# One layer of a hybrid encoder on one core: PSUM tiles cut to single banks, first head loads, combination steps and fillers re-timed

## The chip, the core and the metric

The kernel runs on one core of one Trainium2 chip. The metric is device time in microseconds of one launch; the kernel before has a median of 1358.91 us over three runs (1358.9 to 1362.09). The engines are called by the names of the profile: PE (matmuls; PEld is its weight load), DVE, ACT, POOL, and SP, whose queue SPq issues every DMA of this kernel (all go through one helper, line 119, in the order in which the program names them).

## The reference

For 1024 tokens and a model width of 1024 (fp32):

```python
h = rmsnorm(x)
proj = h @ w_in                       # split into mla | dilated q, k, v, z | gates
a_out = mla_attention(...)            # 8 heads, full softmax over 1024 keys
y_mla = (a_out * silu(z_mla)) @ w_o_mla
d_out = dilated_mixture(...)          # 3 groups x 8 heads, windows (128,1), (512,4), (2048,16)
y_dil = (d_out * silu(z_dil)) @ w_o_dil
merged = sigmoid(g_mla + b) * y_mla + sigmoid(g_dil + b) * y_dil
out = rmsnorm(x + merged @ w_out)
```

In the dilated mixture the three groups' outputs of one head are added with weights that come from a softmax over their log-denominators. That weighting is called the combination below.

## The kernel before, in words

Every fp32 product is made of three fp32r products of a high and a low part: `mm3` (lines 122 to 125) issues them, and `split` (lines 127 to 130) makes the parts, high on ACT, low on POOL or DVE.

**Stages.** Up to 528 us of the profiled execution the kernel computes the normed input, the latents, the values of the dilated heads, and then, in `blocks`, sixteen blocks of projections (queries, keys, and four gate blocks at the end). A block has seven places of 12 matmuls, each 128x128 by 512 columns; places are counted by `x`, and a block's steps on DVE, ACT and SP run on for up to six places past its last one. The four tiles of the last gate block are stored behind its last place. Then follow the dilated stage and the MLA stage in `attention` and `mla_attention`, and the output stage in `output`.

**Dilated stage.** There are four pairs of heads; a pair has 18 units: 8 of group 0, 8 of group 1 and 2 of group 2, so 72 units, one for each turn `t` of the loop in `attention` (lines 1234 to 1268). Turn `t` issues, in this order: transpositions of unit t, scores and maxima of unit t+2, the low part of t, fillers, exponentials of t+2, the result of t-2 (DVE reads the accumulated values out of PSUM, line 1106 or 1181), fillers, and the values product of t-1 (line 1087 for group 1, line 1080 for group 0, line 1175 for group 2). The loads of the next head stand in the same order. After a pair's last unit its combination runs in steps that are hung on later turns (dictionary at the end of `combine`, read with key k as: turn of the last unit plus 2 plus k): statistics (-1), a reload by token from DRAM (0), differences (3), exponents and factors (4), quotients and their store (5), reloads of the quotients spread over the partitions (6 and 7), and weighted products (7, 8, 9), whose sums POOL adds (line 1343). The result is stored to DRAM (`s_da`). The three sums of a pair live in a ring `num` of four buffers, so that the second pair's group 1 gets the buffer of the first pair's sum.

**Fillers.** Between attention steps PE does independent work from a generator: `gate_fill`, 16 tiles of gate or z projections with two jobs of 8 steps each (256 steps, a step is 3 matmuls of 512 columns), then `proj_fill`, the branch projections, jobs of 4 steps. `feed(n)` adds n to what is owed and takes whole steps. `FIRST_FEED` steps come ahead of the loop, `DIL_FEED[g]` is fed twice a turn. In `gate_fill` DVE reads a job's bank (line 691) at the first step of the next job; in `proj_fill` right behind the job's last step (lines 762 and 764).

**MLA stage.** 32 units of four ticks, 128 ticks `t` with c = t % 4. Each tick issues four transpositions (line 822), their copy on ACT (824) and the low part on DVE (830); ticks with c of 0 and 1 issue the next unit's scores and maxima, ticks with c of 2 and 3 feed fillers. The last pair's combination runs on in the first ticks. Pieces of the dilated branch (load of sum and z, product at line 974, split) run one every two ticks from tick 11 to 27; only then may the projection fillers begin.

**Banks.** PSUM's eight banks are four tiles of one bank (two for transpositions `pt`, two for fillers `pj`) and two tiles of two banks, whose halves serve as ring `s_ps` (dilated scores) and ring `av2` (dilated values); MLA uses the two wide tiles whole as scores. At the end of the dilated stage `pj` shrinks to the first of its banks, and the other accumulates MLA's values.

**Memory.** After `blocks` the left part of SBUF is placed by hand. `open_areas` claims it in eight areas, each by a one-element memset on POOL (line 1192) that waits for the tiles that lay there; the first instruction of every engine that writes into an area waits for its memset. Areas 0 to 5 were the operand sums of the blocks, area 7 covers all that lay above, among it the tiles from which the last gates are stored. The first two heads' loads are issued at the head of `attention`.

Of the kernel before, what the change touches and what calls it, by code (L numbers as in the profile page):

```python
# [30 lines left out]
FIRST_FEED = 4  # L31
DIL_FEED = (1.43, 1.43, 2.5, 2)
# [8 lines left out]
LEFT, RIGHT = 5632, 134656  # L41

# [12 lines left out]
class Net:  # L55
    def __init__(self, tc, a):
        self.tc, self.nc, self.a = tc, tc.nc, a
        self.owed = 0.0
# [15 lines left out]
    def rings(self, right):  # L74
# [19 lines left out]
        put("brd", 92160, 4096, 7)  # L94
        for name, k in (("zg_z", 0), ("zg_t", 2), ("gate", 0), ("br_x", 2)):
            self.places[name] = [right[:, 512 * (k + i):512 * (k + i) + 512] for i in range(2)]
        b = self.banks
        self.places.update(pt=b[0:2], pj=b[2:4], s_ps=b[4:6], av2=b[6:8], s_mla=self.wide, m_av=b[3:4])
        self.turn = dict.fromkeys(self.places, 0)
# [521 lines left out]
    def blocks(self, items, tp, pp):  # L621
# [12 lines left out]
        with self.tc.manual_schedule():  # L634
            for x in range(1, places + 14):
# [16 lines left out]

                if j == places - 9:
# [28 lines left out]
    def gate_fill(self):  # L682
# [18 lines left out]
        for n, i in enumerate(ZG):  # L701
            w = self.split_weights.pop(n)
            for half in range(2):
# [15 lines left out]
                yield  # L719
        run_all(tail)  # L720

    def proj_fill(self):
# [12 lines left out]
        coming = gate(0)  # L735
# [3 lines left out]
        for n, (i, dt, half) in enumerate(jobs):  # L739
# [8 lines left out]
            t, coming = coming, gate(n + 1)  # L748
# [14 lines left out]
            else:  # L763
                v.scalar_tensor_tensor(out=t, in0=t, scalar=1.0, in1=ps, op0=ALU.add, op1=ALU.mult)  # L764
# [103 lines left out]
    def mla_factors(self, k):  # L868
# [7 lines left out]
        d = self.ep.tile([128, 2, 4], F32, name="m_d", bufs=2)  # L876
        v.tensor_scalar(out=d, in0=self.stats[pair][1][:, :, 4 * half:4 * half + 4], scalar1=2.0, scalar2=None, op0=ALU.mult)
        v.reciprocal(out=d, in_=d)
        tp = self.get("pt")
# [33 lines left out]
    def mla_tick(self, k, c):  # L913

        self.mla_transposes(k, c)
        if c == 0:
# [3 lines left out]
            self.mla_copied(k - 1)  # L920
            self.mla_maxima(k + 1, 0)
# [14 lines left out]
        else:  # L936
# [5 lines left out]
            if c == 2:  # L942
                self.mla_merged(k - 1, self.nc.gpsimd)
                self.mla_gated(k)
            else:
                self.mla_factors(k + 1)

    def mla_attention(self, later, first):

        nc = self.nc  # L950
        held = {}
        for t in range(128):
            k, c = divmod(t, 4)
            if t == 24:
                run_all(self.fill)
                self.fill = self.proj_fill()
                self.owed = 0.0
            self.rate = 1.8 if t < 24 else 1.55 if t < 112 else 3.0
            if t >= 112:
                while self.jobs_done < 16:  # L960
                    next(self.fill)
            self.mla_tick(k, c)
            for f in later.pop(first + t, []):
                f()
            n = t - 11
            if 0 <= n < 16 and n % 2 == 0:
# [634 lines left out]
```

## Time and profile before

| what | us |
|---|---|
| median of three runs | 1358.91 |
| the profiled execution's own time | 1358.58 |
| its span in the trace | 1356.7 |
| PE busy / DVE / ACT / POOL | 1243.8 / 745.6 / 625.7 / 554.7 |
| first, last transposition of the dilated stage | 548.2, 868.0 |
| first, last transposition of the MLA stage | 885.6, 1210.4 |

In a row of the timeline stand the start, the duration, engine, line, operation, output and inputs, and in brackets the idle time before it with what ended it. In a row of the waits stand the waiting instruction, what it waited for, the total, the number of times and the longest. In a row by windows stand the window, its length, each engine's busy time with its count of instructions, the granted TensorE clock (1.00 is full), and the share and GB/s of the DMA engines. The DMA issues give the size of one and the median time to its landing.

### The profile page before, as it was taken

To read this page: it belongs to the slowest core of one execution; us is meant where nothing else is said; L and a number is where in the kernel's file an instruction comes from. 1 tells how busy PE (TensorE), PEld (TensorE's weight loads), DVE (VectorE), ACT (ScalarE), POOL (GpSimd) and SP (SyncE) were. 2 spreads that over 40 slices of the span, in tenths; PEclk is the share of its full clock that TensorE was granted. 3 is DMA by queue.
4 is the path that set the end of the run, shared out by engine and by line. 5 is a ranking of instruction groups with operands and counts; after the bars stand their busy time and mean duration, and the time that the engine had idled before them with its cause. 6 is when DMAs were issued, how large, how long until landed. Compare 5 with 4: busy or idle time off the path is not lost.

```text
span 1356.7 us, 19579 instructions
## 1 busy us (share of the span) xinstructions
PE 1243.8 (92%) x6909; PEld 1077.3 (79%) x6909; DVE 745.6 (55%) x1360; ACT 625.7 (46%) x1304; POOL 554.7 (41%) x448
## 2 busy tenths in 40 slices
PE   8989999999999996999798897978899999997997
PEld 8989998888888885888687786866787878875776
DVE  7563534766576432556657556475566666653332
ACT  7434354434443442655445454344455555643221
POOL 2251259777777673343532302212210111169321
PEclk9999999999999998999899998998899999998999
DMA  9857673465466424877668767725533334235231
GB/s 336 256 174 267 241 241 128 118 175 143 128 161 166 127 102 139 220 186 189 187 167 215 203 174 197 177 76 163 163 86 104 98 80 117 71 132 171 82 136 47
DMA packets 132609, 215.08 MB, mean 159 GB/s; under 512 B 36952, under 2 KB 67488, under 8 KB 128608
## 3 DMA queue, kind: packets, MB, share of 16 engines
q1 hardware_dynamic: 132512, 213.85, 54.5%
q8 instruction: 54, 0.88, 0.3%
q14 instruction: 43, 0.35, 0.1%
HBM read 146.62 MB, written 67.18 MB: 158 GB/s over the span
## 4 chain that ended last, share of the span: by engine, by line
PE 65%; DMA 10%; DVE 10%; POOL 5%; ACT 4%; issue 4%; SPq 2%; ACTq 0%; DVEq 0%; POOLq 0%
PE bank L123 8%; PE bank L125 7%; PE bank L124 7%; PE bank L822 3%; PE st_a L123 2%; PE st_a L125 2%; PE st_a L124 2%; PE st_d L123 2%; PE st_c L123 2%; PE st_d L124 2%; PE st_c L124 2%; PE st_d L125 2%; PE st_c L125 2%; PE pj L123 2%; PE pj L124 2%
## 5 line engine op out<-in xcount | busy, mean ns | idle before, releaser
L130 POOL TENSOR_TENSOR w_l<-w_raw,w_h 128x512 fp32r<-128x512 f32 x192 | 249.1, 1312 | 319.9 <-ACT w_h L129 265.1
L123 PE MATMUL bank<-at_r,w_h 128*128 128x512 f32 x384 | 162.6, 423 | 20.5 <-DVE zt L764 9.8
L129 ACT CAST w_h<-w_raw 128x512 fp32r<-128x512 f32 x192 | 114.8, 622 | 106.0 <-POOL w_raw L474 94.9
L125 PE MATMUL bank<-at_r,w_l 128*128 128x512 f32 x384 | 154.3, 402 | 1.3 <-POOL w_l L130 1.3
L124 PE MATMUL bank<-at_r,w_h 128*128 128x512 f32 x384 | 154.4, 402 | 0.0
L830 DVE TENSOR_TENSOR at_r<-bank,at_r 128x512 fp32r<-128x512 f32 x128 | 88.3, 690 | 104.0 <-ACT at_r L824 103.8
L824 ACT CAST at_r<-bank 128x512 fp32r<-128x512 f32 x128 | 74.9, 586 | 89.8 <-PE bank L822 89.2
L123 PE MATMUL bank<-at_r 96*128 96x512 f32 (+2 forms) x264 | 109.1, 413 | 6.9 <-ACT bank L1418 6.2
L123 PE MATMUL pj<-w_h,at_r 128*128 128x256 f32 x384 | 108.9, 284 | 0.0
L124 PE MATMUL pj<-w_l,at_r 128*128 128x256 f32 x384 | 108.8, 283 | 0.0
L125 PE MATMUL pj<-w_h,at_r 128*128 128x256 f32 x384 | 108.7, 283 | 0.0
L123 PEld LDWEIGHTS bank<-at_r,w_h 128*128 128x128 f32 x384 | 75.0, 195 | 38.2 <-DVE at_f L762 11.8
L125 PE MATMUL bank<-at_r 96*128 96x512 f32 (+2 forms) x264 | 103.6, 393 | 0.0
L124 PE MATMUL bank<-at_r 96*128 96x512 f32 (+2 forms) x264 | 103.1, 391 | 0.0
L1042 DVE CUSTOM_DVE_ANT_0 at_f<-bank,masks 128x256 f32<-128x256 f32 x128 | 49.0, 420 | 97.8 <-PE bank L1033 97.6
L125 PEld LDWEIGHTS bank<-at_r,w_l 128*128 128x128 f32 x384 | 74.8, 195 | 19.6 <-POOL w_l L130 2.5
L806 DVE TENSOR_REDUCE m_nm<-bank 128x1 f32<-128x1024 f32 x64 | 78.1, 1220 | 10.9 <-PE bank L125 8.6
L474 POOL TENSOR_TENSOR w_raw<-w_raw 128x512 f32<-128x512 f32 x64 | 83.7, 1308 | 0.0
L124 PEld LDWEIGHTS bank<-at_r,w_h 128*128 128x128 f32 x384 | 75.2, 196 | 10.5
L1049 ACT ACTIVATE at_f<-at_f,at_f 128x256 f32<-128x256 f32 x128 | 64.3, 504 | 39.4 <-DVE at_f L1042 39.3
L822 PE MATMUL bank<-consts,at_f 128*128 128x128 f32 x512 | 80.0, 280 | 1.1 <-ACT at_f L814 1.1
L814 ACT ACTIVATE at_f<-bank,m_nm 128x1024 f32<-128x1024 f32 x64 | 71.7, 1120 | 11.5 <-DVE m_nm L806 11.5
(283 smaller groups left out, 3172.6 us busy)
## 6 DMA issues: line engine op xcount, KB each, us to landing
w_raw<-wt SPq DMA_DIRECT2D x48, 512.0 KB, 3.7
at_r<-s_dq SPq DMA_DIRECT2D x32, 512.0 KB, 7.4
s_dq<-dq_st SPq DMA_DIRECT2D x80, 128.0 KB, 2.4
s_dk<-dq_st SPq DMA_DIRECT2D x80, 128.0 KB, 2.3
s_dv<-dv_st SPq DMA_DIRECT2D x32, 256.0 KB, 4.5
zt<-s_gt SPq DMA_DIRECT2D x32, 256.0 KB, 3.1
w_raw<-wv SPq DMA_DIRECT2D x12, 512.0 KB, 5.5
at_f<-s_rr SPq DMA_DIRECT2D x48, 128.0 KB, 3.1
```

What stands on the lines that cost most here:

```text
L123: mm(out, lh, rh, start=start, stop=False, skip_group_check=skip)
L124: mm(out, lh, rl, start=False, stop=False, skip_group_check=skip)
L125: return mm(out, ll, rh, start=False, stop=stop, skip_group_check=skip)
L129: self.nc.scalar.copy(out=h, in_=raw)
L130: sub.tensor_tensor(out=l, in0=raw, in1=h.bitcast(F32), op=ALU.subtract)
L474: self.nc.gpsimd.tensor_tensor(out=b[out], in0=b[x], in1=b[y], op=ALU.subtract)
L806: self.nc.vector.tensor_reduce(out=nm, in_=self.s[k, b], axis=AX.X, op=ALU.max, negate=True)
L814: self.nc.scalar.activation(out=p, in_=self.s.pop((k, b)), func=AF.Exp, bias=nm, accum_out=den)
L822: self.nc.tensor.transpose(pt[:, o:o + 128], self.P[k, b][:, 128 * kc:128 * kc + 128], self.ident)
L824: self.nc.scalar.copy(out=h, in_=pt)
L830: self.nc.vector.tensor_tensor(out=l, in0=pt, in1=h.bitcast(F32), op=ALU.subtract)
L1049: nc.scalar.activation(out=p, in_=p, func=AF.Exp, scale=-1.0, bias=nm, accum_out=den)
```

## The change

- The two wide PSUM tiles become four tiles of one bank (`banks_of`); for MLA's scores they are closed and opened anew as two tiles of two banks, and for the output again as single banks.
- The first two heads' loads, and the memsets of areas 0 to 6, are issued inside `blocks`, behind place `places - 1`, ahead of the last block's gate stores. The rest of the memory is claimed in three areas instead of one; the exponentials' ring `p` lies in the first of them.
- `num` becomes a ring of three for groups 0 and 2 and one buffer of its own for group 1.
- Combination steps 3, 4, 5, 6 move one turn ahead (2, 3, 4, 5); steps 7 to 9 stay. For the last pair the steps behind 0 fall on MLA ticks 3, 5, 7, 9, 13, 15 and 17 instead of 2 to 8; its sum isn't stored and reloaded.
- The pieces of the branch get ticks of their own (`PIECES`), with the load three ticks ahead of the product and the split one tick behind it.
- Fewer fillers in the dilated stage (`DIL_FEED`), two more ahead of it; in MLA the rest is spread evenly over ticks 0 to 26, and the projections over ticks 31 to 111. From the end of the dilated stage on a feed ends at a job's end (`one_bank`). The kept `pj` bank is the one used last.
- MLA's reciprocals are transposed one tick later (`mla_spread`), and the product with them (`mla_gated`) one tick later too.
- Projection gates are loaded three jobs ahead instead of one, and in the output stage DVE adds the two branches instead of POOL.

```diff
-FIRST_FEED = 4
-DIL_FEED = (1.43, 1.43, 2.5, 2)
+FIRST_FEED = 6
+DIL_FEED = (1.33, 1.33, 2.3, 1.8)
+LAST_STEPS = {2: 4, 3: 6, 4: 8, 5: 10, 7: 14, 8: 16, 9: 18}
+PIECES = (2, 0, 0), (4, 0, 1), (16, 3, 0), (16, 3, 1), (20, 1, 0), (22, 1, 1), (24, 2, 0), (26, 2, 1)
+GATES_END, PROJ_BEGIN = 27, 31
+AREAS = (0, 8192, 16384, 24576, 32768, 40960, 49152, 65536, 77824, 88064, 120832)
...
     def feed(self, n):
         self.owed += n
         while self.owed >= 1:
             self.owed -= 1
-            next(self.fill, None)
+            self.steps += 1
+            if next(self.fill, None) and self.one_bank:
+                return
...
-        put("pt0", 71680, 9728, 2)
-        put("d_st", 91136, 384, 2)
-        put("p", 92160, 2048, 3)
-        put("num", 98304, 4096, 4)
+        put("p", 71680, 2048, 3)
+        put("d_st", 77824, 512, 2)
+        put("pt0", 78848, 9728, 2)
+        self.places["num"] = [102400, 110592, 98304]
+        put("num1", 106496, 4096, 1)
...
+    def banks_of(self, side, n, size):
+        old = self.open_banks.pop(side, None)
+        if old:
+            old.close()
+        self.open_banks[side] = ExitStack()
+        pool = self.open_banks[side].enter_context(self.tc.tile_pool(name=f"more_{side}{size}{n}", reuse_waits="tile", bufs=1, side=side, space=PSUM))
+        return [pool.tile([128, size], F32, name=f"{side}{size}{i}") for i in range(n)]
...
+                if x == places - 1:
+                    self.close_sums()
+                    self.open_areas(0)
+                    for it in self.items[:2]:
+                        it[0]()
+                        it[1]()
...
-                yield
+                yield True
...
-        coming = gate(0)
+        coming = [gate(i) for i in range(3)]
...
-            t, coming = coming, gate(n + 1)
+            coming.append(gate(n + 3))
+            t = coming.pop(0)
...
-                nc.gpsimd.tensor_tensor(out=m1, in0=t, in1=m1, op=ALU.add)
+                (nc.gpsimd if self.one_bank else v).tensor_tensor(out=m1, in0=t, in1=m1, op=ALU.add)
             self.jobs_done = n + 1
-            yield
+            yield True
...
         v.reciprocal(out=d, in_=d)
+    def mla_spread(self, k):
+        if not self.ends_half(k):
+            return
...
         tp = self.get("pt")
         nc.tensor.transpose(tp[:8, :128], d.rearrange("p h b -> p (h b)"), self.ident)
...
             self.mla_copied(k - 1)
+            self.mla_spread(k)
...
             if c == 2:
                 self.mla_merged(k - 1, self.nc.gpsimd)
-                self.mla_gated(k)
             else:
+                self.mla_gated(k)
                 self.mla_factors(k + 1)
...
+            put(t, load)
+            put(t + gap, product)
+            put(t + gap + 1, parts)
...
-            if t == 24:
+            if t == GATES_END:
                 run_all(self.fill)
+                self.fill = iter(())
+            if t == PROJ_BEGIN:
+                self.brd_done = True
                 self.fill = self.proj_fill()
...
-            self.rate = 1.8 if t < 24 else 1.55 if t < 112 else 3.0
+                if t < GATES_END:
+                    self.rate = max(0, whole - self.steps) / ahead(GATES_END)
+                elif t < 112:
+                    self.rate = max(0, 64 - self.steps) / ahead(112)
+                else:
+                    self.rate = 3.0
...
-        for it in items[:2]:
-            it[0]()
-            it[1]()
...
             if t == N + 1:
+                self.places["s_mla"] = self.places["s_mla"] + self.banks_of("left", 1, S)
...
             if t == N:
-                self.places["pj"] = self.places["pj"][:1]
+                b = self.places["pj"]
+                i = (self.turn["pj"] - 1) % 2
+                self.places["pj"], self.places["m_av"] = [b[i]], [b[1 - i]]
+                self.one_bank = True
+                self.places["s_mla"] = self.banks_of("right", 1, S)
...
-                        later.setdefault(t + 1 + k, []).append(f)
+                        later.setdefault(t + 1 + (k if t < N or k < 1 else LAST_STEPS[k]), []).append(f)
...
-            if half and 2 in gs:
+            if half and 2 in gs and pair < 3:
                 self.dma(self.da[pair], nums[0])
-        return {-1: statistics, 0: by_token, 3: differences, 4: lambda: (exponents(), factors()), 5: quotients,
-                6: lambda: (spread(0, range(3)), spread(1, (0, 1))),
+        return {-1: statistics, 0: by_token, 2: differences, 3: lambda: (exponents(), factors()), 4: quotients,
+                5: lambda: (spread(0, range(3)), spread(1, (0, 1))),
```

More of the change, by code (lines that the diff above doesn't have):

```diff
@@ L72, in hand, with rings @@
         return self.placed[key]
-    def rings(self, right):
+    def rings(self):
         self.places = {}
@@ L950, in mla_attention, with piece, load, product @@
         nc = self.nc
-        held = {}
+        tasks = {}
+        put = lambda t, f: tasks.setdefault(t, []).append(f)
+        def piece(t, j, half, gap=3):
+            x = slice(512 * half, 512 * half + 512)
+            o = {}
+            def load():
+                o["z"] = self.get("bc")
+                self.dma(o["z"], self.zs[4 + j][:, x])
+                if j < 3:
+                    o["y"] = self.get("br_x")
+                    self.dma(o["y"], self.da[j][:, x])
+                else:
+                    o["y"] = self.last_sum[0][:, x]
+            def product():
+                nc.vector.tensor_tensor(out=o["y"], in0=o["y"], in1=o["z"], op=ALU.mult)
+            def parts():
+                self.split(o["y"], self.brd[0][j][:, x], self.brd[1][j][:, x], nc.gpsimd)
+            put(t, load)
+            put(t + gap, product)
+            put(t + gap + 1, parts)
+        for t, j, half in PIECES:
+            piece(t, j, half)
+        whole = len(ZG) * 16
         for t in range(128):
             k, c = divmod(t, 4)
-            if t == 24:
+            if t == GATES_END:
                 run_all(self.fill)
+                self.fill = iter(())
+            if t == PROJ_BEGIN:
+                self.brd_done = True
                 self.fill = self.proj_fill()
-                self.owed = 0.0
-            self.rate = 1.8 if t < 24 else 1.55 if t < 112 else 3.0
+                self.owed, self.steps = 0.0, 0
             if t >= 112:
                 while self.jobs_done < 16:
+                    self.steps += 1
                     next(self.fill)
+            if c >= 2:
+                ahead = lambda end: sum(x % 4 >= 2 for x in range(t, end))
+                if t < GATES_END:
+                    self.rate = max(0, whole - self.steps) / ahead(GATES_END)
+                elif t < 112:
+                    self.rate = max(0, 64 - self.steps) / ahead(112)
+                else:
+                    self.rate = 3.0
             self.mla_tick(k, c)
@@ L1097, in result @@
                 if g not in nums:
-                    nums[g] = self.get("num", [128, S])
+                    nums[g] = self.get("num1" if g else "num", [128, S])
                 y = x["av"][0][0:64], x["av"][1]
@@ L1372, in first @@
             xs[t] = x, self.ep.tile([128, 3], F32, name="o_ss", bufs=4)
-        self.places["pj"] = [self.banks[i] for i in (2, 4, 5, 6, 7)]
+        pj, av = self.places["pj"], self.places["m_av"]
+        more = [x for side in ("left", "right") for x in self.banks_of(side, 2, 512)]
+        self.places["pj"] = pj + more
         self.mla_values(31, 3)
@@ L1396, in output @@
         nc.gpsimd.tensor_scalar(out=gf, in0=gf, scalar1=-1.0, scalar2=None, op0=ALU.mult)
-        self.places["pj"] = [self.banks[i] for i in (3, 0, 1, 2, 4, 5, 6, 7)]
+        self.places["pj"] = av + self.banks[0:2] + pj + more
         todo = [(t, 0, 0, 512) for t in range(4)] + [(t, 1, 512, 1024) for t in range(4)]
@@ L1522, in run @@
             self.brd_done, self.brm_done, self.jobs_done, self.wout_raw = False, [False, False], 0, []
-            self.pt0 = [self.get("pt0", [128, 19 * 128], F32R) for _ in range(2)]
             self.fill = self.gate_fill()
             with tc.manual_schedule():
-                self.open_areas()
-                first = len(nc.cur_bb.bb.instructions)
+                self.open_areas(1)
                 self.attention()
                 self.output()
-                self.order_areas(first)
+                self.order_areas()
+            for x in self.open_banks.values():
+                x.close()
 def _layout(inputs):
```

91 lines of the change are left out of this document (49 added, 42 removed).

## Prediction

> **What bounds the kernel now.** I read the page first, then windows cut at the stages' borders, then PE's waits in each stage, then the timeline around the longest of them.
>
> ```profile
> span 1356.7 us, 19579 instructions
> ```
> ```profile
> 400.00:500.00 100.00, 100.00 (x443) 82.84 (x442) 51.59 (x82) 44.55 (x86) 72.75 (x58) 1.00 0.47 135
> 541.00:885.00 344.00, 308.63 (x1813) 268.02 (x1814) 193.53 (x485) 169.47 (x434) 108.87 (x96) 0.95 0.74 192
> 885.00:981.00 96.00, 77.53 (x399) 64.91 (x397) 59.28 (x88) 46.06 (x83) 21.16 (x16) 0.84 0.45 127
> 981.00:1170.00 189.00, 176.66 (x1079) 154.06 (x1078) 124.39 (x163) 106.08 (x192) 24.31 (x19) 1.00 0.37 98
> ```
>
> In the block stage (first row) PE has no gap: it sets the time, and the change leaves it alone but for its end. In the dilated stage (541 to 885), MLA's first 31 ticks (885 to 981) and the rest, PE is idle for 35.4, 18.5 and 12.3 us, and the first two also show a lowered clock. No other engine is over 66% busy there, so what is lost is lost to waits of PE, and what shortens a wait shortens the kernel, as long as nothing else stands right behind it.
>
> ```profile
> PE bank L1087 <- DVE at_f L1106: 27.3, 14, 6.3
> PE bank L1032 <- DMA at_r<-s_dk: 10.5, 1, 10.5
> PE bank L1032 <- DVE at_f L1042: 5.0, 4, 2.2
> PE bank L1175 <- DVE at_f L1181: 1.7, 3, 0.9
> ```
>
> These are PE's waits from 541 to 885. The first is odd: a values product waits for DVE's result of a unit two turns back, which lies in the other bank of `av2`. Both banks are halves of one tile, so the wait is one for the tile.
>
> **Prices.** A filler step is 3 matmuls of 512 columns; 443 such matmuls take 100 us in the first window, so a step is 0.677 us. An MLA tick without fillers: ticks 31 to 111 fill 981 to 1170; less 64 steps (43.3) 176.66 leaves 133.4 us for 81 ticks, 1.65 us each.
>
> **A, the hand-over to the first heads.**
>
> ```profile
> 516.70 14.03 SPq L119 DMA_DIRECT2D s_gt<-dq_st  x5
> 521.02 0.16 POOL L1192 MEMSET left<- 1x1 f32 x3
> 525.49 0.15 POOL L1192 MEMSET left<- 1x1 f32 x3 [2.63 <-PE st_c L125]
> 530.86 1.15 SPq L119 DMA_DIRECT2D at_r<-s_dq  x2
> 532.64 0.09 POOL L1192 MEMSET left<- 1x1 f32 x1 [7.00 <-DMA s_gt<-dq_st]
> 541.33 0.55 PE L1032 MATMUL bank<-at_r,at_r 128*128 128x256 f32 x1 [10.47 <-DMA at_r<-s_dk]
> ```
> ```profile
> 548.82 0.59 ACT L1064 CAST at_r<-bank 128x512 fp32r<-128x512 f32 x1 [1.28 <-PE bank L1056]
> 554.74 0.59 ACT L1064 CAST at_r<-bank 128x512 fp32r<-128x512 f32 x1 [0.86 <-PE bank L1056]
> ```
> ```profile
> 540.00:550.00 10.00, 8.67 (x35) 7.44 (x36) 2.96 (x14) 3.38 (x11) 0.00 (x0) 0.67 1.07 258
> ```
> ```profile
> at_r<-s_dq SPq DMA_DIRECT2D x10, 512.0 KB, 7.4
> at_r<-s_dk SPq DMA_DIRECT2D x6, 288.0 KB
> at_r<-s_dv SPq DMA_DIRECT2D x2, 576.0 KB, 9.4
> s_gt<-dq_st SPq DMA_DIRECT2D x5, 256.0 KB, 2.0
> ```
>
> The first areas are open at 521.0, but SP stands behind the gate stores until 530.9. Ahead of them, the first head's five loads go out from about 521.2. From first issue to first product took 541.33 - 530.86 = 10.5 us, so the product could start at 531.7. The blocks and six steps ahead of the loop end at 530.9 + 2 x 0.68 = 532.2: PE's wait of 10.47 us is gone, and two more steps ride in it. What is late next are the gate stores: they now stand behind both heads' loads, 2 x (2 x 512 + 2 x 288 + 576) KB = 4.5 MB, which at the 258 GB/s of that window take 17 us, up to about 540, and their own 4 x 256 KB some 4 more. Area 9 (transposed exponentials, results) opens only when they have landed, about 545, and the first ACT copy would come 3 to 4 us sooner than its 548.82. But PE does four turns' scores and fillers meanwhile, and the third copy (554.74 now) needs only the first copy and one pair of exponentials. If the stores overtake, the whole 10.5 us and some of the 0.67 clock come back. Gain 3 to 12; I take **7**, between, nearer the queue, since a 576 KB load lands 9.4 us after its issue behind the others and a 256 KB store on an empty queue in 2.0. The Trainium skill ("DMA: Bandwidth & Descriptors", Queues, rings and completion order) says that each DMA engine takes descriptors in ring order, which speaks against the whole gain; by it alone A would be 3 to 7, by transfers that overtake 10 to 12.
>
> **B, steps taken from the dilated loop.** 76 turns, two feeds each: 237.8 steps before (66 turns x 2.86, 9 x 5, one of 4), 220.6 after. 17.2 x 0.677 = **11.6** less, as far as PE sets a turn's length. Bounds 4 (PE only where no wait is near) and 11.6.
>
> **C, the dilated waits.**
>
> ```profile
> 634.08 0.67 DVE L1106 TENSOR_TENSOR at_f<-bank,at_f 64x512 f32<-64x512 f32 x1
> 637.33 0.21 DVE L1306 COPY at_f<-at_f 16x128 f32<-16x128 f32 x1 [0.87 <-DMA at_f<-s_sd]
> 656.08 0.69 DVE L1341 TENSOR_TENSOR at_f<-at_f,at_f 128x512 f32<-128x512 f32 x1 [1.22 <-DMA at_f<-s_rr]
> 664.21 4.76 POOL L1343 TENSOR_TENSOR at_f<-at_f 128x512 f32<-128x512 f32 x3
> 671.96 1.05 DVE L1106 TENSOR_TENSOR at_f<-bank,at_f 64x512 f32<-64x512 f32 x1 [3.58 <-DMA s_da<-at_f]
> 673.06 1.23 PE L1087 MATMUL bank<-at_r,at_r 128*128 128x256 f32 x4 [6.32 <-DVE at_f L1106]
> ```
> ```profile
> DVE at_f L1341 <- DMA at_f<-s_rr: 11.1, 9, 2.2
> DVE at_f L1106 <- DMA s_da<-at_f: 9.3, 3, 3.6
> ```
> ```profile
> 650.00:675.00 25.00, 16.97 (x88) 14.48 (x89) 16.01 (x38) 10.07 (x28) 13.57 (x13) 0.82 0.69 204
> ```
>
> The longest wait is a chain: a quotient lands late, DVE multiplies late, POOL adds, the sum is stored, DVE's next result waits for the store since it takes over that buffer, and PE waits for DVE because of the shared tile. The own tiles cut the last link (PE would wait for the low part instead, which DVE did earlier), `num1` cuts the store (9.3 us of DVE; it must only wait for POOL's second add, about 667.4), and the spread one turn earlier cuts most of 11.1. The price: the differences, one turn earlier, stand behind the reload of the statistics. DVE would reach them at 634.75, the reload lands at about 637.3: 2.6 us in place of 0.87, three times, with maxima and low part of the next turn queued behind. They are needed two turns later, so I count half, 4 us. Left of 34.0 (27.3 + 5.0 + 1.7): the 5.0 for DVE's burst, these 4, and 3 for late quotients. Gain 34 - 12 = **22**, bounds 10 (the banks alone) and 32. The clock: 0.95 over 344 us is 17 us lost, much of it while PE was idle anyhow; I take **4**, bounds 0 and 8. The Trainium skill ("TensorE: Matmul & The Clock Gate", Part 1) says an idle window of about 3.4 us halves the clock; the 0.82 beside the 6.32 us wait agrees, and three such waits brought under it would by that rule give 3 x 1.7 = 5 in place of 4.
>
> **D, MLA's first 31 ticks.**
>
> ```profile
> PE bank L880 <- DVE m_d L878: 4.1, 2, 2.2
> PE bank L123 <- DVE zt L691: 2.1, 1, 2.1
> ACT at_r L129 <- DVE zt L974: 12.1, 6, 4.2
> ```
> ```profile
> 908.98 1.38 DVE L1341 TENSOR_TENSOR at_f<-at_f,at_f 128x512 f32<-128x512 f32 x2 [4.11 <-DMA at_f<-s_rr]
> ```
>
> Own work: 31 x 1.65 + 15 steps x 0.677 = 61 us; the stage takes 96, so 35 are waits and low clock. It now gets 30 steps, 10.2 us more. Three jobs end there with a single `pj` bank; the pause doesn't help gate jobs, whose bank is read only at the next job's first step, so each costs 2.1 (row L691), 6.2 in all. The wider spacing takes off the 4.11 of DVE and its followers, ACT's 12.1 before the splits and PE's 4.1 for the reciprocals; ticks 27 to 30 have no filler. I leave 20 of the 35: 61 + 10 + 20 = 91, gain **5**, bounds -8 and 14.
>
> **E, MLA from tick 31.**
>
> ```profile
> PE bank L123 <- DVE at_f L762: 8.6, 9, 1.4
> PE bank L880 <- DVE m_d L878: 3.7, 4, 1.7
> PE bank L123 <- DVE zt L764: 3.5, 3, 1.4
> ```
>
> These waits (981 to 1212) come where a feed starts the next job in the bank that DVE still has to read, and where the reciprocals are transposed at once. The pause puts a tick's other PE work between; the later transposition finds them done. Of 15.8 I take **12**, bounds 6 and 15.
>
> **F, output.** PE waits 6.3 us for line 764 and DVE 10.2 for the gates in
>
> ```profile
> PE bank L123 <- DVE zt L764: 6.3, 4, 3.0
> DVE zt L764 <- DMA zt<-s_gt: 10.2, 5, 3.6
> ```
>
> Earlier gate loads and the add off POOL: **3**, bounds 0 and 7.
>
> **Sum.** 7 + 11.6 + 22 + 4 + 5 + 12 + 3 = 64.6 off the profiled execution's 1358.58 (span 1356.7 and 1.9 around it; the runs' median is 0.3 above it): **1294**.
>
> **Rivals.** *The waits move*: DVE, in order, stalls on the statistics as long as it stalled on quotients, and the stores hold up area 9. Left: 3 + 11.6 + 10 - 5 + 9 = 28.6, so 1330. For it: every wait in C hangs on a DMA's landing. Against: two of the three landings get a turn more or fall away. *All waits go*: 11 + 11.6 + 30 + 7 + 12 + 14 + 6 = 91.6, so 1267; against it stands DVE's burst of small operations, which nothing shortens. *The tiles don't do what they say*: reopened on the same banks, they wait as before; C loses 10, 1304. *Slower*: the dilated turn is paced by the chain scores, maxima, exponentials, copy, low part, values, and the fillers only fill what it leaves. Then fewer steps and shorter PE waits give nothing there, and in MLA, paced alike, 15 steps (10.2) and three job ends (6.2) come on top, less 3 from A: 1358.6 + 13.4 = 1372. It decides if PE's idle time in the dilated stage grows by as much as B removes. Against: PE is 90% busy there.
>
> **How the numbers follow.** Forecast 0.52 (its own range 1276 to 1314), tiles 0.08, waits move 0.22, all go 0.11, slower 0.05, 0.02 for no change. A difference under 0.3% (4 us) can't be told from none. Range 1266 to 1336: outside are the slower case, no change, and the far sides of the two neighbours. Faster 0.92, same 0.03, slower 0.05.
>
> **What would show it.** Right: no PE wait over 4 us between 528 and 550; line 1087 gone from PE's waits; no DVE wait on `s_da`; line 1306 waiting 2 to 3 us; clock at 0.97 or more in the dilated stage; under 4 us of PE waits on lines 762 and 764 in MLA. Wrong: more PE idle time in the dilated stage than 25 us, or 100 us and more for MLA's first 31 ticks.

## The result, and the profile after

| | us | ratio to before, 95% interval |
|---|---|---|
| before, median of four runs | 1359.58 (1358.9 to 1362.09) | |
| after, median of four runs | 1293.18 (1291.12 to 1295.12) | 0.9508 (0.9488 to 0.9528) |
| the profiled execution after | 1295.12, span 1293.1 | |

The forecast was 1294. To see whether its terms hold too, both spans are cut at the same instructions: the end of the blocks' matmuls, the first transposition of the fourth dilated unit (the hand-over ends there), that of the last dilated unit, and those of MLA's ticks 0, 31, 112 and 127. The later experiments stand in the same table.

| stage, us | ahead | hand-over | dilated | to MLA | ticks 0-31 | 31-112 | 112-127 | tail | span |
|---|---|---|---|---|---|---|---|---|---|
| before | 528.1 | 30.1 | 309.4 | 17.9 | 95.0 | 189.6 | 39.9 | 146.6 | 1356.7 |
| after | 531.2 | 28.1 | 269.5 | 20.0 | 90.7 | 182.5 | 35.1 | 136.1 | 1293.1 |
| one_tile_dil | 526.6 | 27.5 | 294.8 | 20.4 | 87.1 | 181.7 | 35.1 | 137.3 | 1310.6 |
| banks_alone | 528.2 | 30.2 | 283.9 | 17.6 | 94.6 | 189.6 | 40.0 | 137.8 | 1321.8 |
| one_tile_out | 530.6 | 28.8 | 271.4 | 20.4 | 90.3 | 184.1 | 35.2 | 146.4 | 1307.1 |
| num_ring | 527.7 | 27.7 | 276.9 | 20.0 | 88.9 | 184.4 | 35.1 | 135.4 | 1296.0 |
| old_steps | 526.6 | 28.2 | 268.1 | 20.4 | 87.9 | 183.9 | 35.1 | 138.4 | 1288.6 |
| old_feed | 531.0 | 28.1 | 276.6 | 16.9 | 81.9 | 180.5 | 35.1 | 136.6 | 1286.7 |
| loads_late | 532.2 | 20.7 | 268.5 | 20.4 | 90.3 | 184.0 | 35.1 | 135.9 | 1287.1 |
| second_late | 532.0 | 18.5 | 270.4 | 20.4 | 90.9 | 184.6 | 35.1 | 137.8 | 1289.7 |
| no_pause | 533.6 | 28.9 | 274.0 | 19.5 | 85.8 | 192.1 | 40.2 | 132.7 | 1306.9 |
| gate_read | 527.3 | 27.0 | 270.1 | 17.9 | 79.5 | 181.9 | 35.1 | 137.4 | 1276.3 |
| both | 528.9 | 18.9 | 269.8 | 18.8 | 78.5 | 184.3 | 35.2 | 135.0 | 1269.4 |
| both_feed | 529.0 | 19.2 | 277.9 | 16.9 | 72.6 | 183.4 | 35.2 | 137.0 | 1271.3 |

Each line is one execution. What the same code gives in different lines is the scatter: 526.6 to 533.6 ahead of the blocks' end, where almost nothing was changed, and some 2 us either way in the other stages. (The line of no_pause is the slowest of its four runs, 8 us over the next.) So a stage is read from this table, a whole kernel from its median and ratio. Differences between two variants are given below by their ratios, times 1359.

From before to after, the dilated stage gave 39.9 us, the ticks from 31 on 11.9, the tail 10.5, the first 31 ticks 4.3 and the hand-over 2.0, 68.6 in all; the blocks' end came 3.1 later, which is within the scatter, and the way to MLA took 2.1 more, so 63 us are left. The windows answer to those of the prediction. The first fence is the dilated stage of before, cut as in the table; in the second, of after, stand the hand-over, the dilated stage, ticks 0 to 31 and the rest of MLA:

```profile
558.20:867.60 309.40, 275.18 (x1643) 239.75 (x1642) 180.98 (x454) 156.76 (x401) 103.51 (x92) 0.96 0.74 191
```
```profile
531.00:554.00 23.00, 14.46 (x75) 11.78 (x74) 5.49 (x19) 5.90 (x18) 1.93 (x5) 0.91 1.06 248
559.30:828.80 269.50, 256.58 (x1598) 227.80 (x1597) 176.70 (x452) 154.15 (x399) 101.27 (x91) 0.98 0.82 210
848.80:939.50 90.70, 79.45 (x434) 68.07 (x433) 61.51 (x87) 46.31 (x83) 22.89 (x17) 0.92 0.44 120
939.00:1157.00 218.00, 211.05 (x1295) 185.56 (x1295) 148.53 (x194) 129.78 (x234) 43.23 (x34) 1.00 0.40 110
```

In the dilated stage PE's idle time falls from 34.2 us (309.40 less 275.18) to 12.9, and its busy time by 18.6, with 45 matmuls fewer (15 steps, 10.2 us by the price of the prediction) and the clock at 0.98 for 0.96. Of the 18.6 us of busy time 8.4 are left beside the 10.2 of the matmuls; they go with the higher clock. MLA's first ticks still lose 11.3 us and still run at a lowered clock. In the hand-over PE is idle for 8.5 of 23 us. PE's waits name the causes: the first line below lies in the hand-over, the next three in the dilated stage, the fifth in ticks 0 to 31, the last two behind them.

```profile
PE bank L1121 <- DVE at_r L1133: 7.4, 1, 7.4
...
PE left L1152 <- DVE at_r L1133: 4.6, 3, 2.2
PE right L1097 <- DMA at_r<-s_dk: 4.0, 2, 3.2
PE bank L1121 <- DVE at_r L1133: 3.2, 4, 1.8
...
PE bank L143 <- DVE zt L718: 9.7, 3, 4.2
...
PE bank L143 <- DVE at_f L790: 3.2, 7, 0.9
PE bank L143 <- DVE zt L792: 0.4, 1, 0.4
```

Line 1152 is the values product of group 1 (1087 before). It no longer waits for the result of a unit two turns back, but for its own input, the low part (line 1133), and for 4.6 us in place of 27.3. The scores (line 1097, before 1032) no longer wait for DVE's maxima of the other bank, 5.0 us before, but for a load of keys. Lines 718, 790 and 792 are the old 691, 762 and 764.

The hand-over is where the profile contradicts the prediction. The timeline shows why: SP's issues, then POOL's memset that opens area 9, ACT's first copy and PE's third set of transpositions. Two groups of the DMA issues between 530 and 540 follow (in each the landing of one is known), and the window from the first load to the landing of the second head's keys.

```profile
524.56 1.13 SPq L139 DMA_DIRECT2D at_r<-s_dq  x2
525.78 1.50 SPq L139 DMA_DIRECT2D at_r<-s_dk  x2
...
530.98 1.18 SPq L139 DMA_DIRECT2D at_r<-s_dk  x2
533.49 0.38 SPq L139 DMA_DIRECT2D at_r<-s_dv  x1
534.77 7.50 SPq L139 DMA_DIRECT2D s_gt<-dq_st  x4
...
552.10 0.09 POOL L1260 MEMSET area<- 1x1 f32 x1 [19.99 <-DMA at_r<-s_dq]
552.22 0.59 ACT L1129 CAST at_r<-bank 128x512 fp32r<-128x512 f32 x1 [11.11 <-POOL area L1260]
...
553.68 1.09 PE L1121 MATMUL bank<-consts,at_f 128*128 128x128 f32 x4 [7.39 <-DVE at_r L1133]
```
```profile
at_r<-s_dq SPq DMA_DIRECT2D x2, 512.0 KB, 13.7
s_gt<-dq_st SPq DMA_DIRECT2D x1, 256.0 KB, 15.2
```
```profile
524.50:547.00 22.50, 20.64 (x102) 16.81 (x100) 7.53 (x20) 6.52 (x15) 0.36 (x6) 1.00 1.02 221
```

The loads do go out early, and PE's wait for the first keys is down from 10.47 to 1.2 us. But the four gate stores stand behind all ten loads: the first is issued at 534.77 and lands 15.2 us later, at 549.97, where before a store landed 2.0 us after its issue. The memset lies under them and runs at 552.10, where in the kernel before it ran at 532.64. (The name in its bracket is a load of the same queue; the memset's place under the stores is the program's.) ACT's first copy comes at 552.22. That is 21.0 us behind the blocks' end, as before (548.82, 20.7 behind), so nothing is won, and PE, with two banks for transpositions, stops for 7.39 us.

Last, two of DVE's waits from 531 to 849, for the combination's reloads:

```profile
DVE at_f L1417 <- DMA at_f<-s_rr: 11.8, 7, 4.1
DVE at_f L1382 <- DMA at_f<-s_sd: 7.0, 3, 3.5
```

No wait for `s_da` is left. But the quotients (line 1417, before 1341) are waited for as long as the 11.1 us of before, and the statistics' reload (line 1382, before 1306) for 7.0.

### The profile page after: what moved, and what is told of

Read it like the earlier page. It is cut to its first block, busy times and chain, and to the rows that moved or that the text cites. A ratio compares the mean times of both kernels' runs of the same rounds, so it can differ in the third digit from the quotient of the medians.

```text
span 1293.1 us, 19574 instructions
## 1 busy us (share of the span) xinstructions
PE 1225.1 (95%) x6909; PEld 1070.9 (83%) x6909; DVE 765.7 (59%) x1371; ACT 624.8 (48%) x1304; POOL 542.0 (42%) x439
## 4 chain that ended last, share of the span: by engine, by line
PE 72%; DMA 11%; DVE 7%; issue 3%; POOL 3%; SPq 2%; ACT 2%; DVEq 0%; ACTq 0%; POOLq 0%
PE bank L143 5%; PE bank L145 5%; PE bank L144 5%; PE pj L143 4%; PE pj L144 4%; PE pj L145 4%; PE bank L850 3%; PE st_a L143 2%; PE st_a L145 2%; PE st_a L144 2%; PE st_c L143 2%; PE st_d L143 2%; PE st_c L145 2%; PE st_d L145 2%; PE st_c L144 2%
## 5 line engine op out<-in xcount | busy, mean ns | idle before, releaser
L143 PE MATMUL bank<-at_r,w_h 128*128 128x512 f32 x348 | 146.7, 422 | 15.7 <-DVE zt L718 11.6
L145 PE MATMUL bank<-at_r,w_l 128*128 128x512 f32 x348 | 139.6, 401 | 0.8 <-POOL w_l L150 0.8
L144 PE MATMUL bank<-at_r,w_h 128*128 128x512 f32 x348 | 139.7, 402 | 0.0
L143 PEld LDWEIGHTS bank<-at_r,w_h 128*128 128x128 f32 x348 | 67.6, 194 | 28.8 <-DVE zt L718 12.7
L1107 DVE CUSTOM_DVE_ANT_0 at_f<-right,masks 128x256 f32<-128x256 f32 x128 | 48.9, 418 | 59.1 <-PE right L1098 59.0
L145 PEld LDWEIGHTS bank<-at_r,w_l 128*128 128x128 f32 x348 | 67.4, 194 | 16.7 <-POOL w_l L150 1.2
L144 PEld LDWEIGHTS bank<-at_r,w_h 128*128 128x128 f32 x348 | 67.8, 195 | 9.3
L144 PEld LDWEIGHTS pj<-w_l,at_r 128*128 128x128 f32 x384 | 74.6, 194 | 0.8
L143 PEld LDWEIGHTS pj<-w_h,at_r 128*128 128x128 f32 x384 | 74.4, 194 | 0.9
L145 PEld LDWEIGHTS pj<-w_h,at_r 128*128 128x128 f32 x384 | 74.5, 194 | 0.7
L875 PE MATMUL bank<-at_r,at_r 128*128 128x256 f32 x256 | 67.9, 287 | 2.8 <-DVE at_r L858 2.8
L874 PE MATMUL bank<-at_r,at_r 128*128 128x256 f32 x256 | 68.1, 286 | 0.1
```

Source lines behind the costliest of these rows:

```text
L143: mm(out, lh, rh, start=start, stop=False, skip_group_check=skip)
L144: mm(out, lh, rl, start=False, stop=False, skip_group_check=skip)
L145: return mm(out, ll, rh, start=False, stop=stop, skip_group_check=skip)
L874: mm(out, vv[:, kc], ph[:, x], start=kc == 0, stop=False)
L875: mm(out, vv[:, kc], pl[:, x], start=False, stop=kc == 7)
```

## Experiments

All but banks_alone are the kernel after with one edit, or with the edits named. Where the edit undoes a part of the change, what the run takes beyond after is what that part was worth; second_late, gate_read, both and both_feed repair something instead. Line numbers differ from those of after by up to three, those of banks_alone from before by up to twelve.

### Own banks in the dilated stage

```diff
-                self.places["av2" if side == "left" else "s_ps"] = self.banks_of(side, 2, 512)
+                w = self.banks_of(side, 1, S)[0]
+                self.places["av2" if side == "left" else "s_ps"] = [w[:, 0:512], w[:, 512:1024]]
```

> The changed kernel with one undo: the dilated stage's score ring and value ring are again the two halves of one two-bank tile each; everything else stays. Theory (the shared tile makes a values product wait for DVE's result in the other bank, whatever else is mended): the waits of the group 1 values product on DVE's result come back, 8 to 12 us in all in the dilated stage, and the time rises from 1293 to about 1303. Rival (the own banks matter little, since the long waits ended with the freed buffer and the earlier steps): at most 3 us more, 1293 to 1296.

Measured: 1316.63, ratio 0.9693 (0.9668 to 0.9718), 25 us over after. All of it lies in the dilated stage, 294.8 for 269.5. The largest of PE's waits there:

```profile
PE left L1152 <- DVE at_f L1171: 21.9, 16, 4.0
PE right L1097 <- DVE at_f L1107: 8.8, 7, 1.7
```

These are the two waits of before, under new line numbers. The first is the odd one: a values product waits for DVE's reading of the other bank. With nothing but the tiles changed it is back, so the wait was one for the tile. The second is the same in the scores' ring: a unit's scores wait for DVE's maxima of the unit in the other bank. The mechanism was expected; the size is two and a half times what I gave it. In the other direction, only the banks were added to the kernel before:

```diff
-        self.places.update(pt=b[0:2], pj=b[2:4], s_ps=b[4:6], av2=b[6:8], s_mla=self.wide, m_av=b[3:4])
+        self.places.update(pt=b[0:2], pj=b[2:4], s_ps=self.banks_of("left", 2, 512), av2=self.banks_of("right", 2, 512), s_mla=[], m_av=b[3:4])
...
+                self.places["s_mla"] = self.places["s_mla"] + self.banks_of("right", 1, S)
...
+                self.places["s_mla"] = self.banks_of("left", 1, S)
...
-        self.places["pj"] = [self.banks[i] for i in (2, 4, 5, 6, 7)]
+        more = [x for side in ("left", "right") for x in self.banks_of(side, 2, 512)]
+        self.places["pj"] = [self.banks[2]] + more
```

> The kernel before with one part of the change alone: the two two-bank tiles become four tiles of one bank, reopened as two-bank tiles for MLA's scores and as single banks for the output; loads, buffers, steps, feeds and pauses stay as before. Theory (the shared tiles cost 25 us in the dilated stage and 10 in the output, whatever stands beside them): 1322 to 1328 against 1359 for the kernel before, with MLA unchanged. Rival (a part of the 25 us comes only with the freed buffer and the moved steps, since the long waits then still end on the stored sum): 10 to 15 us less in the dilated stage, 10 in the output, 1334 to 1340.

Measured: 1318.8, ratio 0.9697 (0.9667 to 0.9728): 41 us less than before, by this part alone, more than expected. The dilated stage falls from 309.4 to 283.9 and the tail from 146.6 to 137.8; MLA is as before. The dilated stage's row:

```profile
558.40:842.30 283.90, 269.68 (x1643) 239.16 (x1642) 179.55 (x454) 155.83 (x401) 103.62 (x92) 0.97 0.80 207
```

With the same 1643 matmuls as before, PE is idle for 14.2 us in place of 34.2. Undone or done alone, the banks are worth 25 us in the dilated stage.

### Own banks in the output stage

```diff
-        more = [x for side in ("left", "right") for x in self.banks_of(side, 2, 512)]
+        more = [w[:, 512 * i:512 * i + 512] for side in ("left", "right") for w in self.banks_of(side, 1, S) for i in range(2)]
```

> The changed kernel with one undo: in the output stage the four further banks are again halves of two two-bank tiles. Theory (four of the waits at the end, 1.54 us each, were a matmul's wait for ACT in the other half): PE's waits on ACT's squares are back, about 6 us in all, and the time is 1298 to 1300. Rival (the output stage's gain of 10.5 us comes from DVE's add and the earlier gate loads): 1293 to 1294.

Measured: 1307.77, ratio 0.959 (0.9553 to 0.9628), 11 us over after and more than the 1298 to 1300 expected; the tail is 146.4, as long as before. The largest of PE's waits in the output stage of before, then of this kernel:

```profile
PE bank L123 <- DVE zt L764: 6.3, 4, 3.0
PE bank L123 <- ACT bank L1418: 6.2, 4, 1.5
```
```profile
PE right L143 <- DVE zt L792: 4.4, 2, 3.6
PE right L143 <- ACT right L1497: 3.1, 2, 1.5
PE left L143 <- ACT left L1497: 3.1, 2, 1.5
```

The second row of before is what I had passed over: four waits of 1.5 us for ACT's squares in the final norm (line 1418, now 1497). They are the tile's wait again, since PE starts in one half while ACT still writes its squares into the other. The first row of before was largely the tile's as well: the waits for DVE's product of the branches (line 764, now 792) are back too, with nothing but the tiles changed, while after has 0.4 us of them. DVE's addition of the branches and the earlier gate loads, from which I had expected the gain, are in this kernel, and it gains nothing; banks_alone has neither, gains 8.8, and there DVE still waits for the gates as it did before (10.2 us):

```profile
DVE zt L773 <- DMA zt<-s_gt: 10.0, 4, 3.6
```

So that wait of DVE costs at most the 1.7 us by which the tails of banks_alone and after differ. The two edits were not run by themselves.

### A buffer of its own for group 1's sum

```diff
-        self.places["num"] = [102400, 110592, 98304]
-        put("num1", 106496, 4096, 1)
+        put("num", 98304, 4096, 4)
...
-                    nums[g] = self.get("num1" if g else "num", [128, S])
+                    nums[g] = self.get("num", [128, S])
```

> The changed kernel with one undo: the three sums of a pair lie again in one ring of four buffers, so that the next pair's group 1 takes over the buffer whose contents are stored to DRAM. Theory (the store's landing was one link of the chain): DVE's wait for the store is back, three times about 3.5 us, and since PE no longer waits for DVE's result itself but only for what DVE does behind it, about half shows: 1297 to 1300. Rival 1 (the store was the whole of the long waits): three times 5 us, 1308. Rival 2 (own banks alone have cut the chain): 1293.

Measured: 1300.7, ratio 0.9584 (0.9561 to 0.9606), 10 us over after, just over the 1297 to 1300 expected; 7.4 of it in the dilated stage. DVE's wait for the store is back, longer than the 9.3 us of before:

```profile
DVE at_f L1170 <- DMA s_da<-at_f: 12.3, 3, 5.5
```

### Combination steps one turn earlier

```diff
-LAST_STEPS = {2: 4, 3: 6, 4: 8, 5: 10, 7: 14, 8: 16, 9: 18}
+LAST_STEPS = {3: 4, 4: 6, 5: 8, 6: 10, 7: 14, 8: 16, 9: 18}
...
-        return {-1: statistics, 0: by_token, 2: differences, 3: lambda: (exponents(), factors()), 4: quotients,
-                5: lambda: (spread(0, range(3)), spread(1, (0, 1))),
+        return {-1: statistics, 0: by_token, 3: differences, 4: lambda: (exponents(), factors()), 5: quotients,
+                6: lambda: (spread(0, range(3)), spread(1, (0, 1))),
```

> The changed kernel with one undo: the combination's differences, factors, quotients and reloads are back at steps 3, 4, 5 and 6 for the first three pairs (the last pair keeps its new places). Theory (the reload of the quotients lands too late for the products): DVE's waits on that reload are back at about 3 us a pair, its wait at the differences falls from 2 or 3 us to under 1, and the time rises by 4 to 6 us to 1297 to 1299. Rival (the stall only moved from the quotients to the statistics): no change, 1292 to 1294.

The first two lines keep the last pair's ticks. Measured: 1290.75, ratio 0.9511 (0.9487 to 0.9534): the same time as after. DVE's waits for the two reloads in the dilated stage:

```profile
DVE at_f L1417 <- DMA at_f<-s_rr: 14.6, 9, 3.1
DVE at_f L1382 <- DMA at_f<-s_sd: 1.7, 3, 0.9
```

Together 16.3 us, against 18.8 in after: the earlier steps take 2.8 us off the wait for the quotients and put 5.3 on that for the statistics. The rival, that the stall only changes its place, was right.

### Fewer fillers in the dilated stage

```diff
-FIRST_FEED = 6
-DIL_FEED = (1.33, 1.33, 2.3, 1.8)
+FIRST_FEED = 4
+DIL_FEED = (1.43, 1.43, 2.5, 2)
```

> The changed kernel with one undo: 4 filler steps ahead of the dilated loop and the old shares in it, so 15 steps (10.2 us of matmuls) move back from MLA's first ticks. Theory (PE sets the length of a dilated turn, and MLA's first ticks are full too): the dilated stage grows by 10 to 12 us, MLA's first 31 ticks shrink by 10 and by two job ends of 2 to 4 us each, so the sum is 1287 to 1294. Rival 1 (the dilated turn is paced by its chain, fillers only fill): the dilated stage stays, MLA shrinks, 1280 to 1284. Rival 2 (MLA's first ticks had room): the dilated stage grows, MLA stays, 1303.

Measured: 1286.11, ratio 0.9475 (0.9452 to 0.9498). With the old fillers the kernel is not slower but 4.5 us faster, though the two intervals overlap by 0.001. The table shows both sides: the dilated stage takes 7.1 us more, the way to MLA 3.1 less and the first 31 ticks 8.8 less. A step taken out of the dilated stage comes back where PE has less cover for it. So this part of the change, 7.1 us by its own stage, was no gain to the kernel.

### The first heads' loads

```diff
-                    for it in self.items[:2]:
-                        it[0]()
-                        it[1]()
...
         items, units, ends = self.items, self.dil_units, self.ends
+        for it in items[:2]:
+            it[0]()
+            it[1]()
```

> The changed kernel with one undo: both first heads' loads are issued again at the head of the attention stage, behind the last gate stores; the memsets that open the memory stay where the change put them. Theory (early loads only trade a wait for loads against a wait for the gate stores that stand behind them): PE again waits about 9 us for the first keys, but the 7.4 us wait of the third unit's transpositions goes; unit 3 starts 28 to 31 us behind the blocks' end instead of 28.1, and the time is 1293 to 1296. Rival (the early loads earn their 10 us): 1300 to 1303.

Measured: 1288.48, ratio 0.946 (0.9438 to 0.9482), 6.5 us less than after, against the expectation. The timeline of SP shows that this is no pure undoing:

```profile
525.21 1.14 SPq L139 DMA_DIRECT2D at_r<-s_dq  x2
526.43 1.19 SPq L139 DMA_DIRECT2D at_r<-s_dk  x2
531.58 1.51 SPq L139 DMA_DIRECT2D s_gt<-dq_st  x3
533.53 0.38 SPq L139 DMA_DIRECT2D at_r<-s_dv  x1
```

The last block's late steps run beside the head of `attention`, and in the order that came out the first head's queries and keys still go ahead of three gate stores, its values and the second head behind them. That points at the second head, so it alone was held back:

```diff
-                    for it in self.items[:2]:
-                        it[0]()
-                        it[1]()
+                    self.items[0][0]()
+                    self.items[0][1]()
...
         items, units, ends = self.items, self.dil_units, self.ends
+        items[1][0]()
+        items[1][1]()
```

> The changed kernel with one part moved: only the first head's loads are issued inside the block stage; the second head's go out at the head of the attention stage, behind the last gate stores. Theory (the gate stores stand behind 4.4 MB of loads, and the last memory area opens when they land): the stores land about 9 us sooner, the wait of the third unit's transpositions falls from 7.4 us to under 1, unit 3 starts 20 to 22 us behind the blocks' end instead of 28.1, and the time is 1285 to 1288; the second head's keys come just in time. Rival 1 (the stores are held up by something else): no change, 1293. Rival 2 (the second head is then too late at unit 4): the gain is given back at the fifth unit, 1291 to 1294.

Measured: 1285.59, ratio 0.9448 (0.9418 to 0.9479), 8 us less than after, within the expectation. (In the order that came out one load of the second head still goes ahead of the last store.) The memset of area 9 in its timeline:

```profile
541.63 0.09 POOL L1259 MEMSET area<- 1x1 f32 x1 [8.70 <-PE right L1097]
```

The last store, issued at 534.25, had landed 7.1 us later, at 541.32; the name in the bracket is that of a matmul that ran meanwhile. The memset comes 10.5 us sooner than in after, the hand-over takes 18.5 us in place of 28.1, and PE waits 0.5 us for the keys. So the early loads could give 11.6 us; both heads' loads ahead of the stores give back all but 2.

### The pause at a job's end

```diff
-            if next(self.fill, None) and self.one_bank:
-                return
+            next(self.fill, None)
```

> The changed kernel with one undo: a feed no longer ends at a job's end when one bank is left for the fillers. Theory (a second job begun in the same feed waits for DVE's read of the bank): in MLA from tick 31 to 127 PE's waits on that read rise from 3.6 us to 10 to 13, and the time to 1300 to 1303. Rival (those waits only stand in for others, MLA is paced by ACT and DVE): under 3 us, 1293 to 1296.

Measured: 1300.05, ratio 0.9568 (0.9533 to 0.9603), 8 us over after, as expected. In the table ticks 31 to 127 take 14.7 us more; the first 31 take 4.9 less and the tail 3.4 less. PE's longest waits in ticks 31 to 127:

```profile
PE bank L142 <- DVE at_f L789: 10.0, 10, 1.8
PE bank L142 <- DVE zt L791: 3.6, 3, 1.4
```

They are the waits of lines 762 and 764 of before, 8.6 and 3.5 us there and 3.2 and 0.4 in after.

### DVE's read at the end of a gate job

The pause does nothing for a gate job, whose bank DVE reads only at the next job's first step. Here the read is issued at the job's end instead, once only one bank is left:

```diff
                 tail = after(i, half, ps)
+                if self.one_bank:
+                    next(tail, None)
                 yield True
```

> The changed kernel with one step moved: from the end of the dilated stage on, DVE reads a gate job's bank right behind the job's last step, not at the first step of the next job. Theory (the pause at a job's end is of no use to gate jobs, whose bank is read only when the next job begins): the three waits of the fillers on that read, 9.7 us in MLA's first 31 ticks, fall to under 2, the 31 ticks take 82 to 85 us instead of 90.7, and the time is 1285 to 1288. Rival (those ticks are paced by ACT and DVE, the waits only fill): 90 us, 1292 to 1294.

Measured: 1282.44, ratio 0.9415 (0.9392 to 0.9438), 13 us less than after, more than expected. Ticks 0 to 31 take 79.5 us, with PE's busy time and the granted clock in the first row (PE's busy time stands behind the length, the clock behind POOL's count), and PE's wait for the read in the second:

```profile
844.40:923.90 79.50, 74.31 (x436) 64.25 (x434) 60.52 (x88) 47.39 (x85) 22.91 (x17) 0.98 0.56 146
```
```profile
PE bank L143 <- DVE zt L718: 3.0, 1, 3.0
```

Against the 90.7 us of after, PE's idle time falls from 11.3 to 5.2 us and its busy time from 79.45 to 74.31, with as many matmuls and the clock at 0.98 for 0.92. So of the 11.2 us, 6.1 were idle time and 5.1 came back by the clock: busy time times clock is 73 us in both.

### The two repairs together

```diff
-                    for it in self.items[:2]:
-                        it[0]()
-                        it[1]()
+                    self.items[0][0]()
+                    self.items[0][1]()
...
+                if self.one_bank:
+                    next(tail, None)
...
+        items[1][0]()
+        items[1][1]()
```

> The changed kernel with two moves: the second head's loads behind the last gate stores, and DVE's read of a gate job's bank right behind the job in MLA. Theory (the two lie in different stages and add): a ratio to the kernel before of 0.935 to 0.937, about 1272 to 1275. Rival (the dilated stage, started 9 us sooner, finds its later loads late): 1279 to 1283.

Measured: 1273.29, ratio 0.9361 (0.9335 to 0.9388), 20 us less than after, as expected: the two add up. With the old fillers as well:

```diff
-FIRST_FEED = 6
-DIL_FEED = (1.33, 1.33, 2.3, 1.8)
+FIRST_FEED = 4
+DIL_FEED = (1.43, 1.43, 2.5, 2)
```

> The same two moves, and 4 filler steps ahead of the dilated loop with the old shares in it, so 15 steps go back from MLA to the dilated stage. Theory (the old shares gained because job ends in MLA cost 2 to 4 us each; with these gone, a step costs about the same in either place): within 3 us of the kernel with the two moves alone. Rival (a dilated turn hides part of its steps, 7 us were seen for 11.6 us of matmuls): 4 to 5 us faster than that kernel, 1268 to 1271.

Measured: 1270.05, ratio 0.9338 (0.9312 to 0.9364), the fastest here, 23 us less than after. That it also beats both, by 3 us, between what was expected and the rival, the intervals don't settle. The table shows the exchange once more, and there it is even: ticks 0 to 31 give 5.9 us and the way to MLA 1.9, the dilated stage takes 8.1.

## Why the prediction was right, and where its terms were not

**The total** came out 0.8 us from the forecast: the stages that were to give the gain gave it. But A, B and F were off by 4 to 8 us each, C was made up otherwise than I had it, and the longer way to MLA had no term. These errors cancelled, so that the total came within 1 us is luck.

| term | foretold | measured | shown by |
|---|---|---|---|
| A, hand-over | 7 (3 to 12) | 2.0 | after, second_late |
| B, fewer steps | 11.6 (4 to 11.6) | 7.1 | old_feed |
| C, dilated waits with clock | 22 + 4 | 25.3 banks, 7.4 `num1`, -1.4 steps | one_tile_dil, num_ring, old_steps |
| D, ticks 0 to 31 | 5 | 4.3 | after |
| E, from tick 31 | 12 | 11.9 | after, no_pause |
| F, output | 3 (0 to 7) | 10.5 | one_tile_out, banks_alone |

**A** failed at a size, the time of the transfers. The stores were named as what is late next, but I let area 9 open at about 545 and it opened at 552.10. Some 3 us of this are the blocks' later end in this execution. The rest is that I moved 4.5 MB at 258 GB/s in 17 us; with a load of weights just ahead of them it was 5.0 MB, and they went at 221 GB/s, until about 547. So the first copy came as late behind the blocks as before instead of 3 to 4 us sooner, and "no PE wait over 4 us between 528 and 550" was wrong. The Trainium skill ("DMA: Bandwidth & Descriptors", Queues, rings and completion order) has each DMA engine take descriptors in ring order; the store's 15.2 us against 2.0 agrees, and what it gave for A by itself, 3 to 7, was nearer than transfers that overtake.

**B and C** are 39.9 us together, against 37.6 foretold, and the four undone parts add up to 38.4. By the rows of the dilated stage the 39.9 are 10.2 of matmuls, 21.3 of idle time and 8.4 that go with the clock, where 11.6, 22 and 4 were foretold. B gained 7.1 in its stage, but old_feed shows that the same steps cost 11.9 on the way to MLA and in its first ticks. The prediction's own prices had that loss: 11.6 against 10.2 for the steps and two more job ends of 2.1 in D.

Inside C, "the banks alone" was my lower bound, 10, and they brought 25: I counted the last link of one long chain. In one_tile_dil, though, the wait stands at each of group 1's 16 banks, at eleven of them (9.9 of 21.9 us) with no late quotient before it. And the 5.0 us that I left standing for DVE's burst were the wait of the scores for their tile: it is gone in after, and 8.8 us in one_tile_dil. The 12 us left over came out at 12.9, but by luck, since 4.0 of them are a load of keys that I had not counted and 8.9 are waits for the low part (line 1133). "The spread one turn earlier cuts most of 11.1" failed: the quotients' waits are 11.8, the statistics' reload costs DVE 7.0, as priced (2.6 three times), and undoing the step changes nothing. There the rival that the waits move was right, for that one edit. The wait of line 1087 for a result of two turns back is gone, as is DVE's for `s_da`, and the clock at 0.98 is over the 0.97 that was asked for. How much of its gain came with which part was not run.

**D** met its 91 us with 90.7, with an inner shift: the three job ends cost 9.7 us, not 6.2, and lower the clock as well. **E** went as foretold; the pause is shown by no_pause, while that the later transposition of the reciprocals removes the 3.7 us of line 880 is read only from the missing row. **F** failed by an oversight: waits of the very kind I had just explained stood in the output stage, one on ACT, which I passed over, and one on DVE, line 764, which I put down to the gate loads and to POOL's addition.

**Of the rivals**, the slower one is refuted, since idle time in the dilated stage fell by 21.3 us, where it would have had to grow. That the tiles don't do what they say is refuted by one_tile_dil.

**Not settled:** the earlier gate loads and DVE's addition, the branch pieces' ticks, the last pair's wider steps, the even spread of the fillers in MLA and the later transposition weren't run by themselves; banks_alone and one_tile_out leave the first two at most some 2 us.

## What to carry to other kernels

When PE waits for a reader of another buffer of the same ring, look at what tile the ring is cut from: two banks in one tile wait for each other, and cutting them apart was worth some 35 of the 66 us here, without one operation less. Having found such a wait, look through every stage for its kind, whichever engine reads. A load that is moved ahead must be paid for by what it now stands in front of: move only what the next product needs, and leave the store that frees memory ahead of the rest.

## What was not expected of the hardware

- A 256 KB store took 2.0 us from issue to landing on the short queue (before), 15.2 as the first of four, which SP took 7.5 us to issue, behind ten loads of 4.5 MB (after), and 5.9 and 7.1 behind about half of them (second_late).
- Three PE waits of 9.7 us in all, the longest 4.2, went with a granted clock of 0.92 over 90 us; with one wait of 3.0 left it was 0.98. The clock's share was 5.1 us beside 6.1 of idle time, so a wait there cost nearly twice its length. The trace gives the clock as full or one half, and one half in stretches of 3.41 us or a multiple. Three stretches of after, behind or within waits of 4.2, 3.4 and 2.1 us, and the one of gate_read, at the end of its wait of 3.0 us:

```profile
870.71:874.12 3.41, 3.41 (x11) 2.79 (x10) 1.55 (x5) 0.00 (x0) 0.00 (x0) 0.50 0.03 7
891.19:898.01 6.82, 5.35 (x17) 4.58 (x18) 1.42 (x4) 1.35 (x3) 1.27 (x1) 0.50 0.78 241
918.49:921.90 3.41, 3.41 (x12) 2.85 (x11) 0.00 (x0) 0.00 (x0) 0.00 (x0) 0.50 0.75 222
```
```profile
862.33:865.74 3.41, 2.84 (x7) 2.28 (x8) 3.34 (x8) 1.18 (x2) 1.28 (x1) 0.50 0.20 77
```

The Trainium skill ("TensorE: Matmul & The Clock Gate", Part 1) gives about 3.4 us of idle time as what halves the clock; as a limit for a single wait this does not agree, since 2.1 and 3.0 us sufficed here. Not every such wait did it: one of 2.5 us behind tick 31 of after brought no lowered clock.
